# Rotary embedding of 16 x 512 x 1024 floats: the last tile stored in two pieces, and three small transfers in place of four

## The chip, the core and the metric

The kernel runs on one core of a Trainium2 chip. The time is device microseconds of one execution. Times inside a run ("at 147.6 us") count from the start of the profiled span, which is some 1.8 us shorter than the time of the run.

A transfer is cut into packets, which 16 DMA engines carry side by side; the last store of the kernel before is 128 packets of 32 KB, eight for each engine. A transfer has landed when each engine, after its packets, has counted up the semaphore of the transfer, a counter that other instructions wait for. A store is issued when SyncE hands it to its queue; its packets move when the engines come to them.

## The reference

```python
def reference(x, cos, sin, num_heads):          # shortened; x: 16 x 512 x 1024 float32, 16 heads of 64
    x = x.reshape(batch, seq, num_heads, head_dim)
    x1, x2 = x[..., :half_dim], x[..., half_dim:]
    # cos, sin: 512 x 32, broadcast over batch and heads
    return np.concatenate([x1 * cos - x2 * sin, x1 * sin + x2 * cos], axis=-1)
```

The input is 33.6 MB and so is the output. Each byte has to be moved once in each direction, 67.1 MB in all.

## The kernel before

The work is cut into eight tiles of 128 partitions. A partition holds eight rows of 1024 floats, so a tile is 4.19 MB. Five tile buffers are loaded at once; the last three loads wait until a buffer has been stored. All loads and stores are issued by SyncE and share one queue. Rows 0 and 3 are added on TensorE and copied by ScalarE; rows (1, 2), (4, 5) and (6, 7) are summed on VectorE in pairs; GpSimd makes the sine products.

```python
FIRST = (2, 3, 8)      # first tile: pieces of 2, 1 and 5 rows
LAST_OUT = (8,)        # last tile: stored whole
EXTRA = 4              # small transfers
...
    load(0, 0, FIRST[0])
    ...                                        # cos and sin tables, on ScalarE's queue
    for lo, hi in zip(FIRST, FIRST[1:]):
        load(0, lo, hi)
    for t in range(1, BUFS):
        load(t)
    spare = fixed.tile([1, EXTRA, 16], FP32)
    for i in range(EXTRA):                     # 64 bytes each, read by nobody
        nc.sync.dma_start(out=spare[:1, i], in_=sin_v[:1, :16])
...
    def stores(t):
        lo = 0
        for hi in LAST_OUT if t == NT - 1 else (KK,):
            store(t, lo, hi)
            lo = hi
        if t + 1 == NT - BUFS:
            for n in range(BUFS, NT):
                load(n)
...
        pair_sum(*p2, b2)                      # rows 4, 5
        pe_half(ROW_PE, *h1)                   # second half of row 3
        p1 = pair_product(t, third[0])         # rows 6, 7
        ...
        pair_sum(*p1, b1)
        stores(t)
```

The small transfers carry nothing that is used. They turn the sequence of semaphores: the transfers use eight semaphores in turn, and a transfer is not issued before the one eight places earlier has landed (in the trace of before the first landed at 5.91 us and the ninth was issued at 5.92).

Of the kernel before, what the change touches and what calls it, by code (L numbers as in the profile page):

```python
# [19 lines left out]
PAIRS = ((1, 2), (4, 5), (6, 7))  # L20

FIRST = (2, 3, 8)
LAST_OUT = (8,)

EXTRA = 4


@with_exitstack
def kernel(
# [40 lines left out]
    def load(t, lo=0, hi=KK):  # L70
        if tiles[t] is None:
            tiles[t] = xp.tile([P, F], FP32, name="xt")
        s = slice(lo * dim, hi * dim)
        nc.sync.dma_start(out=tiles[t][:, s], in_=x_v[t][:, s])

    def store(t, lo=0, hi=KK):
        s = slice(lo * dim, hi * dim)
        nc.sync.dma_start(out=out_v[t][:, s], in_=tiles[t][:, s])
# [9 lines left out]
# [3 lines that stand above are left out]
    for i in range(EXTRA):  # L91
        nc.sync.dma_start(out=spare[:1, i], in_=sin_v[:1, :16])
# [98 lines left out]
# [4 lines that stand above are left out]
# [64 lines left out]
```

## Time and profile before

| | |
|---|---|
| time, median of 3 runs | 162.48 us (162.30 to 162.54) |
| profiled span | 160.4 us |
| last sum on VectorE ends | 147.52 us |
| last store issued, landed | 147.59, 159.57 us |
| the store before it, landed | 149.92 us |
| moved over the span | 67.25 MB, mean 419 GB/s |
| busy share VectorE, GpSimd | 85%, 79% |

On the DMA row a packet's whole duration is booked in the slice in which the packet starts.

### The profile page before, as it was taken

To read this page: it belongs to the slowest core of one execution; us is meant where nothing else is said; L and a number is where in the kernel's file an instruction comes from. 1 tells how busy PE (TensorE), PEld (TensorE's weight loads), DVE (VectorE), ACT (ScalarE), POOL (GpSimd) and SP (SyncE) were. 2 spreads that over 40 slices of the span, in tenths; PEclk is the share of its full clock that TensorE was granted. 3 is DMA by queue.
4 is the path that set the end of the run, shared out by engine and by line. 5 is a ranking of instruction groups with operands and counts; after the bars stand their busy time and mean duration, and the time that the engine had idled before them with its cause. 6 is when DMAs were issued, how large, how long until landed. Compare 5 with 4: busy or idle time off the path is not lost.

```text
span 160.4 us, 444 instructions
## 1 busy us (share of the span) xinstructions
PE 57.0 (36%) x71; PEld 18.1 (11%) x71; DVE 136.3 (85%) x85; ACT 18.7 (12%) x25; POOL 127.1 (79%) x38
## 2 busy tenths in 40 slices
PE   3323705076305830293009320852057203930000
PEld 0102201031002200130004000300021002200000
DVE  1079879999999999999999999999999999997000
ACT  0003301003100310021100310031003100220000
POOL 1059999999999999988998799989989899830000
PEclk9999965556755585559555865567555855595555
DMA  5999999999999999999999999999999999999993
GB/s 176 413 414 469 400 515 392 392 474 441 392 441 449 417 392 458 458 392 433 476 400 425 482 400 400 490 409 400 466 433 409 441 458 409 433 466 409 409 474 163
DMA packets 2761, 67.25 MB, mean 419 GB/s; under 512 B 328, under 2 KB 456, under 8 KB 584
## 3 DMA queue, kind: packets, MB, share of 16 engines
q1 hardware_dynamic: 2600, 67.11, 97.8%
q10 hardware_dynamic: 160, 0.13, 0.3%
q14 instruction: 1, 0.01, 0.0%
HBM read 33.69 MB, written 33.55 MB: 419 GB/s over the span
## 4 chain that ended last, share of the span: by engine, by line
DVE 68%; issue 11%; POOL 7%; DMA 4%; PE 1%; ACTq 0%; DVEq 0%
DVE xt L189 33%; DVE pd L141 31%; POOL b L165 7%; DMA b<-in_cos_dram 4%; DVE pe_ps L141 4%; PE tab L114 1%; ACTq L84 0%; DVE sns L116 0%; DVE xt L150 0%; DVE own_ps L141 0%; DVE sns L117 0%; DVEq L189 0%
## 5 line engine op out<-in xcount | busy, mean ns | idle before, releaser
L165 POOL TENSOR_TENSOR b<-xt,sns 128x2048 f32<-128x2048 f32 (+1 forms) x32 | 126.4, 3978 | 14.0 <-DVE sns L117 8.6
L189 DVE TENSOR_TENSOR xt<-pd,b 128x2048 f32<-128x2048 f32 x24 | 54.9, 2287 | 2.4 <-POOL b L165 1.6
L141 DVE TENSOR_TENSOR pd<-xt,tab 128x2048 f32<-128x2048 f32 x24 | 55.0, 2292 | 0.2
L176 PE MATMUL own_ps<-xt,ident 128*128 128x512 f32 x32 | 30.1, 1095 | 59.4 <-DVE xt L150 53.7
L176 PE MATMUL pe_ps<-b,ident 128*128 128x512 f32 x32 | 24.7, 864 | 22.6 <-DVE pe_ps L141 22.6
L176 PEld LDWEIGHTS own_ps<-xt,ident 128*128 128x128 f32 x32 | 9.4, 324 | 75.2 <-DVE xt L150 60.5
L209 ACT COPY xt<-own_ps 128x1024 f32<-128x1024 f32 x8 | 8.1, 1012 | 78.6 <-PE own_ps L176 78.6
L181 ACT COPY xt<-pe_ps 128x512 f32<-128x512 f32 x16 | 9.4, 586 | 32.8 <-PE pe_ps L176 32.8
L176 PEld LDWEIGHTS pe_ps<-b,ident 128*128 128x128 f32 x32 | 7.4, 253 | 42.9 <-DVE pe_ps L141 34.4
L141 DVE TENSOR_TENSOR pe_ps<-xt,tab 128x512 f32<-128x512 f32 x16 | 11.0, 685 | 0.0
L141 DVE TENSOR_TENSOR own_ps<-xt,tab 128x1024 f32<-128x1024 f32 x8 | 9.8, 1223 | 0.0
L150 DVE TENSOR_TENSOR xt<-xt,tab 128x1024 f32<-128x1024 f32 x8 | 9.7, 1214 | 0.0
L116 DVE TENSOR_SCALAR sns<-tab 128x256 f32<-128x256 f32 x1 | 0.4, 425 | 7.5 <-PE tab L114 7.5
L209 ACT ACT_TABLE_LOAD x1 | 1.3, 1283 | 14.7 <-DVE xt L150 14.7
L113 PE MATMUL tab<-b,spread 64*128 64x256 f32 x2 | 1.2, 697 | 3.4 <-DMA b<-in_sin_dram 3.4
L101 PE MATMUL own_ps<-zero 128*128 128x512 bf16 x2 | 1.0, 622 | 1.2 <-DVE zero L97 1.2
L114 PE MATMUL tab<-b,spread 64*128 64x256 f32 x2 | 1.2, 710 | 0.5 <-DMA b<-in_cos_dram 0.5
L97 DVE MEMSET zero<- 128x256 uint32 x1 | 0.3, 272 | 0.9 <-PEq L240 0.9
L113 PEld LDWEIGHTS tab<-b,spread 64*128 64x128 f32 x2 | 0.5, 310 | 4.3 <-issue 4.3
L114 PEld LDWEIGHTS tab<-b,spread 64*128 64x128 f32 x2 | 0.5, 306 | 1.3 <-DMA b<-in_cos_dram 1.3
L101 PE MATMUL pe_ps<-zero 128*128 128x512 bf16 x1 | 0.6, 634 | 0.0
L101 PEld LDWEIGHTS <-zero 128*128 128x128 bf16 x3 | 0.3, 125 | 1.5 <-DVE zero L97 1.2
(9 smaller groups left out, 1.8 us busy)
## 6 DMA issues: line engine op xcount, KB each, us to landing
out_dram<-xt SPq DMA_DIRECT2D x8, 4096.0 KB, 21.9
xt<-in_x_dram SPq DMA_DIRECT2D x7, 4096.0 KB, 30.0
xt<-in_x_dram SPq DMA_DIRECT2D x1, 2560.0 KB
xt<-in_x_dram SPq DMA_DIRECT2D x1, 1024.0 KB
xt<-in_x_dram SPq DMA_DIRECT2D x1, 512.0 KB
b<-in_sin_dram ACTq DMA_DIRECT2D x1, 64.0 KB, 5.2
b<-in_cos_dram ACTq DMA_DIRECT2D x1, 64.0 KB
spare<-in_sin_dram SPq DMA_DIRECT2D x4, 0.1 KB
```

The source lines that it names most:

```text
L97: nc.vector.memset(zero, 0.0)
L101: nc.tensor.matmul(out=ps, lhsT=zero[:, :P], rhs=zero, start=True, stop=True)
L113: nc.tensor.matmul(out=sin_t, lhsT=spread, rhs=sin_sb, start=True, stop=True)
L114: nc.tensor.matmul(out=cos_t, lhsT=spread, rhs=cos_sb, start=True, stop=True)
L116: nc.vector.tensor_scalar_mul(out=sns[:, :, 0, :], in0=sin_k, scalar1=-1.0)
L141: nc.vector.tensor_tensor(out=o, in0=i, in1=cb, op=ALU.mult)
L150: nc.vector.tensor_tensor(out=heads(r), in0=heads(r), in1=s, op=ALU.mult)
L165: nc.gpsimd.tensor_tensor(out=o, in0=i, in1=sb, op=ALU.mult)
L176: nc.tensor.matmul(out=ps, lhsT=ident, rhs=other, start=False, stop=True, skip_group_check=True)
L181: nc.scalar.copy(out=r, in_=pe_ps)
L189: nc.vector.tensor_tensor(out=r, in0=ps, in1=b, op=ALU.add)
L209: nc.scalar.copy(out=r0, in_=own_ps)
```

## The change

The intent of the split is to let half of the last tile leave when rows 0 to 3 are ready, while the last pair of rows is still being computed. One small transfer is dropped, so that there are again 24 transfers and the last one is again on the last of the eight semaphores.

```diff
 FIRST = (2, 3, 8)
-LAST_OUT = (8,)
-
-EXTRA = 4
+LAST_OUT = (4, 8)
+
+EXTRA = 3
```

## The prediction

> **What bounds the kernel now.** I read the page's span and DMA lines first, because the change only touches transfers.
>
> ```profile
> span 160.4 us, 444 instructions
> ...
> DMA  5999999999999999999999999999999999999993
> ...
> q1 hardware_dynamic: 2600, 67.11, 97.8%
> ...
> DVE 68%; issue 11%; POOL 7%; DMA 4%; PE 1%; ACTq 0%; DVEq 0%
> ```
>
> The DMA row is at 9 in every slice but the first and the last, and the queue that SyncE feeds takes 97.8% of what 16 engines have in the span. The chain that ended last tells another story, 68% VectorE and 4% DMA. These are different questions: the chain follows releases back from the last work on an engine, and no engine's work has to wait for the end of the last store. So I asked when the queue could have run dry. Stretches first (columns: the stretch, its length, busy us of PE, PEld, DVE, ACT and POOL with their counts, PE clock, DMA share, GB/s):
>
> ```profile
> 2.00:147.50 145.50, 56.20 (x70) 17.84 (x68) 135.75 (x83) 18.66 (x25) 126.40 (x32) 0.65 1.00 429
> 147.50:149.90 2.40, 0.00 (x0) 0.00 (x0) 0.03 (x1) 0.00 (x0) 0.00 (x0) 0.50 0.98 423
> ```
>
> From 2 us until the arithmetic ends at 147.5 us the DMA engines are busy all the time, at 429 GB/s, and they still are for the 2.4 us after it. The end of the timeline, then SyncE's line with the store before it (issue at 131.54; two stores merged in one line), then the time from issue to landing of the one and the other, from the list of DMA issues in a window around 131.5 and around 147.6 us:
>
> ```profile
> 140.04 2.29 DVE L189 TENSOR_TENSOR xt<-pd,b 128x2048 f32<-128x2048 f32 x1
> ...
> 144.15 0.59 ACT L181 COPY xt<-pe_ps 128x512 f32<-128x512 f32 x1 [3.05 <-PE pe_ps L176]
> 145.23 2.29 DVE L189 TENSOR_TENSOR xt<-pd,b 128x2048 f32<-128x2048 f32 x1
> 147.59 0.33 SPq L78 DMA_DIRECT2D out_dram<-xt  x1
> ```
> ```profile
> 131.54 16.38 SPq L78 DMA_DIRECT2D out_dram<-xt  x2
> ```
> ```profile
> out_dram<-xt SPq DMA_DIRECT2D x1, 4096.0 KB, 18.4
> ```
> ```profile
> out_dram<-xt SPq DMA_DIRECT2D x1, 4096.0 KB, 12.0
> ```
>
> The store before the last is issued at 131.54 and lands 18.4 us later, at 149.9. The last is issued at 147.59 and lands 12.0 us later, at 159.6. The two landings are 9.7 us apart, and 4.19 MB in 9.7 us is 432 GB/s: the full rate of this queue. So of the 12.0 us, about 2.3 us are queueing behind the store before it, and the rest is movement at full speed. The semaphore records of the trace say the same of every 4 MB transfer: landings at 23.3, 33.0, 42.7, 52.6, 62.4, 72.0, 82.2, 91.9, 101.1, 110.8, 120.5, 130.2, 140.3, 149.9 and 159.6 us, in the order of issue, 9.2 to 10.2 us apart. The packet records of the last two stores have each engine going from one 32 KB packet (1.213 us) to the next with no gap, across the border between the stores, which the engines cross between 148.7 and 149.5 us. The kernel is a **full DMA queue from 1.8 us to 159.6 us**; bytes decide the end.
>
> Last, SyncE's own waits over the whole run:
>
> ```profile
> SPq L78 <- DVE xt L189: 112.2, 7, 16.6
> SPq L74 <- DMA out_dram<-xt: 16.7, 2, 9.7
> SPq L254 <- DMA out_dram<-xt: 11.4, 2, 9.6
> SPq L92 <- DMA xt<-in_x_dram: 5.3, 1, 5.3
> ```
>
> L92 is the small transfers, one of which holds SyncE 5.3 us; L254 is the end of the program, which waits 9.6 us for the last store.
>
> **What the Trainium skill says.** The Trainium skill, "DMA: Bandwidth & Descriptors", section "Queues, rings and completion order": on each engine descriptors are taken in ring order, and all that SyncE issues shares one row of rings. The landings above, all in issue order, agree; so a store issued earlier behind a full queue doesn't start moving earlier than its predecessors leave. Same page, section "Bandwidth": 16 ports at 32 B and 850 MHz give 435 GB/s; the 429 GB/s above is 99% of it, so no reordering can make the middle faster. Same page, "Why small descriptors are slow": a fixed cost for each packet. The packet records agree: 4096 B take 159 ns and 32,768 B take 1213 ns, so 1054 ns for 28,672 B, 0.0368 ns a byte, and 159 - 151 = 8 ns fixed. "Perfetto Trace Analysis", section "DMA Optimizations", says that splitting may let some transfers start sooner "if DMA engines are generally idle". Here they are not, at the one place where the split is made.
>
> **The change part by part.** The description also names the tables on ScalarE's queue and the first tile in pieces of two, one and five rows; both are in the kernel before, and the diff leaves them. Only two constants change.
>
> Last store in two. Rows 0 to 3 of the last tile are ready when the second half of row 3 has been copied: 144.15 + 0.59 = 144.74 us (rows 1 and 2 were summed by 137.1, row 0 copied by 139.9). Rows 6 and 7 are ready at 145.23 + 2.29 = 147.52. So the first piece is issued at about 144.8, 2.8 us earlier than now, and the second at 147.6 as now. But the store before occupies the engines until 148.7 to 149.5 (landing 149.9). The first piece, 2.1 MB, lands at about 149.9 + 4.85 = 154.8, the second at about 159.6. Removed from the end: 0. Added: on each engine 16 packets of 16 KB in place of 8 of 32 KB, so 8 x 8 ns = 0.065 us, and one more 4-byte semaphore packet, which with the step to it costs some 15 ns in the packet records. Together +0.08 us.
>
> One small transfer fewer. The fourth small one waits for the last piece of the first tile, which lands at 13.6 us; that is the 5.3 us wait above. Without it SyncE is free at about 8.3 rather than 13.8 us, and its next order is the first store at 29.7 us, which waits for VectorE. Worth 0. Its own 64 bytes (11 ns on one engine) and semaphore packet go: -0.02 us at most.
>
> Which semaphore each transfer uses moves. The trace shows eight semaphores in turn over all 24 transfers; a transfer waits until the one eight before it has landed. There are again 24 (3 small, 9 stores), so the last transfer again has the last of the eight. Stores 1 to 3 now follow the last piece of tile 0 (13.6), load 1 (23.3) and load 2 (33.0), and are issued at 29.7, 46.7 and 63.6; the loads at 64.1, 72.1 and 82.2 follow load 3 (42.7), load 4 (52.6) and a small one; the later stores follow small ones and stores that landed over 30 us before. The two pieces follow the third store (82.2) and the load that landed at 91.9. Nothing binds: 0.
>
> Sum: 0 + 0.08 - 0.02 + 0 = +0.06 us. On the median of before, 162.48, I take **162.5 us**.
>
> **The rivals.** *The exposed tail.* If one reads the last 12.0 us as a store with nothing beside it, half of it can go 2.8 us earlier and only 2.1 MB remain after 147.6: 4.85 us of movement plus about 2 us of latency, so an end 5 us earlier and some 157.5 us. For it: the digit rows of the engines are empty at the end, and the chain stops at VectorE. Against it: the DMA share of 0.98 from 147.5 to 149.9, the 9.7 us between landings, and above all the bytes: 67.1 MB at 432 GB/s need 155.4 us after a start at 1.8, so 157.2 at the earliest, and the kernel ends 2.4 us over that. Even with everything moved ideally it can't win 2%. I give it 1%.
>
> *A new wait by the moved semaphores.* If I have the turn wrong by one and a load is held until a transfer that is still queued, the queue could run dry: one such hole can cost up to a transfer's 9.7 us, 172 us at worst. Against it: every predecessor named above landed at least 13 us before the issue that would wait for it, with 20 us or more in the loads. 1%.
>
> *Smaller packets lose rate.* If 16 KB packets on the HBM side ran 2% slower, the last store would take 0.2 us more: 162.7. The 20 KB packets of the first tile are at 762 to 766 ns, 26.8 GB/s an engine against 27.0, so a per-cent effect on 4 MB, 0.1 us. Inside my range.
>
> *The queue was only just full.* The fastest engine left the earlier store at 148.7, 1.1 us after the last issue. If unprofiled runs are nearer to running dry, an earlier first piece helps a few tenths: 162.2. Also in the range.
>
> **Range and chances.** The three runs of before lie within 0.24 us, and my terms are under 0.1 us, so what is left is a different chip or hour: 162.1 to 163.0. Two per cent is 3.25 us, more than all of the kernel's DMA idle time together; hence 0.01 faster, 0.98 within 2%, 0.01 slower.
>
> **What would show it.** Right: DMA row all 9 as now; first piece issued near 144.8 and landing about 10 us later, second issued near 147.6 and again landing about 12.0 us later; three waits of the last line on the stores (about 2, 5 and 5 us) in place of two, with much the same sum; the 5.3 us wait of L92 gone and nothing moved by it. Wrong: a landing of the second piece under 10 us after its issue (the tail was exposed), a new wait of L74 or L78 on a DMA, or a DMA slice below 9 in the middle.

## The result

The changed kernel took 162.69 us (median of 6 runs, 162.26 to 162.79). The kernel before took 162.51 us beside it (6 runs, 162.30 to 162.82). The ratio is 1.0003, with a 95% interval of 0.9986 to 1.002: the same. Ratios here are the mean time of one kernel's fast runs over that of the other's of the same rounds, so they are not quite the ratio of the medians quoted.

The page of the changed kernel (span, DMA row, SyncE's queue with packets, MB and share, and the chain):

```profile
span 161.0 us, 444 instructions
...
DMA  5999999999999999999899999999999999999993
...
q1 hardware_dynamic: 2742, 67.11, 97.5%
...
DVE 68%; issue 11%; POOL 6%; DMA 4%; PE 1%; ACTq 0%; DVEq 0%
```

The queue is as full as before: 97.5% against 97.8%, with the same bytes. It has 142 packets more, which come from the 16 KB pieces: 128 data packets and 16 for the semaphore of the added store, less two of the dropped small transfer. The chain still reads 68% VectorE.

The stretches of the changed kernel up to the end of the arithmetic and just after it (the last two columns are DMA share and GB/s):

```profile
2.00:147.50 145.50, 55.74 (x70) 17.79 (x68) 135.55 (x83) 18.56 (x25) 126.43 (x32) 0.65 1.00 430
147.50:149.90 2.40, 0.00 (x0) 0.00 (x0) 0.21 (x1) 0.00 (x0) 0.00 (x0) 0.50 0.94 403
```

The end of the timeline, then SyncE's line of the last three stores:

```profile
145.28 0.59 ACT L181 COPY xt<-pe_ps 128x512 f32<-128x512 f32 x1 [5.14 <-PE pe_ps L176]
145.42 2.29 DVE L189 TENSOR_TENSOR xt<-pd,b 128x2048 f32<-128x2048 f32 x1
```
```profile
131.73 16.34 SPq L78 DMA_DIRECT2D out_dram<-xt  x3
```

The first piece was issued at 145.89 us, as soon as the second half of row 3 had been copied (145.28 + 0.59), and the second at 147.74. Their times from issue to landing, in the windows around 145.5 and around 148 us:

```profile
out_dram<-xt SPq DMA_DIRECT2D x1, 2048.0 KB, 9.4
```
```profile
out_dram<-xt SPq DMA_DIRECT2D x1, 2048.0 KB, 12.4
```

This is the whole result in two lines. The second piece is half the size of the old last store, was issued at the same place in the program, and took 12.4 us to land where the whole store took 12.0. A piece of 2.1 MB needs 4.85 us of movement at 432 GB/s; most of the rest is waiting. By the packet records the engines left the store before at 148.65 to 150.10 us and the first piece at 153.51 to 154.96, so the first piece began to move 2.8 to 4.2 us after its issue and the second 5.8 to 7.2 us after its own. The first piece was issued earlier and stood in the same queue.

SyncE's waits of the changed kernel:

```profile
SPq L78 <- DVE xt L189: 103.6, 7, 21.4
SPq L74 <- DMA out_dram<-xt: 16.6, 2, 9.9
SPq L78 <- ACT xt L181: 13.8, 1, 13.8
SPq L254 <- DMA out_dram<-xt: 11.9, 3, 4.8
```

The wait of 5.3 us for the first tile's last piece (L92) has gone from the list and no load or store has a new wait for a transfer. The end of the program (L254) now waits three times, 11.9 us in all, in place of twice, 11.4 us.

The prediction named a DMA slice below 9 in the middle as a sign against it, and the row above has an 8 in the twentieth slice. I checked it against the packet records. With each packet spread over its own time, every slice but the first and the last is at 1.00 to 1.02, in both kernels, and 16 packets or one more are under way at any moment around that slice. The 8 is the booking by start described above, not idle time.

The profiled run of the changed kernel ends 0.6 us later than that of before (landing at 160.17 against 159.57). The traces give another reason than the change. In both the packets of one of the 16 engines can be followed back from the last landing, and it is the engine that carried the one 8 KB packet of the instruction queue ("q14 instruction: 1" on the page of the kernel before) near 78.6 us: 0.309 us for it, and the data packet after it took 1.571 in place of 1.213 us. In the changed kernel's run this engine lost another 0.43 us in one packet near 109.7 us. Its last packet ended at 159.84, the next engine's at 159.05. In the run of before the two were at 159.21 and 159.04. The lengthened packet near 109.7 is no mark of the change either: the run of before has six packets of 1.29 to 1.47 us near 108.7 to 109.2. Other runs of the changed kernel had the shorter span: 160.5 us in two of six.

The other traces bear this out. In all eight in which the queue stayed full to the end (but for a few ns), the engine that ended last is the one with the instruction packet, 0.2 to 0.8 us after the next. In the three in which the queue ran dry before the last store or its first piece, the last two engines ended within 0.03 us of each other. No run removed that packet, so the link is read from traces and not tested.

### The profile page after: what moved, and what is told of

Its sections match the earlier page's. It is cut to its first block, busy times and chain, and to the rows that moved or that the text cites. A ratio compares the mean times of both kernels' runs of the same rounds, so it can differ in the third digit from the quotient of the medians.

```text
span 161.0 us, 444 instructions
## 1 busy us (share of the span) xinstructions
PE 56.6 (35%) x71; PEld 18.1 (11%) x71; DVE 136.3 (85%) x85; ACT 18.6 (12%) x25; POOL 127.1 (79%) x38
## 3 DMA queue, kind: packets, MB, share of 16 engines
q1 hardware_dynamic: 2742, 67.11, 97.5%
## 4 chain that ended last, share of the span: by engine, by line
DVE 68%; issue 11%; POOL 6%; DMA 4%; PE 1%; ACTq 0%; DVEq 0%
DVE xt L189 33%; DVE pd L141 31%; POOL b L165 6%; DMA b<-in_cos_dram 4%; DVE pe_ps L141 4%; PE tab L114 1%; ACTq L84 0%; DVE sns L116 0%; DVE xt L150 0%; DVE own_ps L141 0%; DVE sns L117 0%; DVEq L189 0%
## 5 line engine op out<-in xcount | busy, mean ns | idle before, releaser
L209 ACT COPY xt<-own_ps 128x1024 f32<-128x1024 f32 x8 | 8.1, 1012 | 78.6 <-PE own_ps L176 78.6
## 6 DMA issues: line engine op xcount, KB each, us to landing
xt<-in_x_dram SPq DMA_DIRECT2D x1, 2560.0 KB, 11.9
```

Of the source, the lines that this page charges most:

```text
L209: nc.scalar.copy(out=r0, in_=own_ps)
```

## Experiments

My theory: the queue is full until after the last store is ready, so only bytes (and the slowest engine) set the end, and moving an issue earlier within a full queue moves nothing. The main rival: the last store is exposed, and the split should win several microseconds, which something in the change then takes back (smaller packets, one more completion, a semaphore wait from the new turn). Nine experiments were run, one of them the changed kernel once more. Eight were made on one chip in two jobs of four; the 12 runs of before beside the second four include the 11 beside the first. The last of the table was made on another chip with runs of before of its own.

| run | median us (runs) | ratio to before | 95% interval |
|---|---|---|---|
| changed kernel again | 162.45 (6) | 1.0007 | 0.9988 to 1.0027 |
| split only | 162.28 (6) | 0.9995 | 0.9978 to 1.0013 |
| three small ones only | 162.32 (6) | 0.9997 | 0.9978 to 1.0015 |
| no small ones | 162.42 (6) | 1.0012 | 0.9988 to 1.0035 |
| late, stored whole | 166.30 (6) | 1.0245 | 1.0204 to 1.0286 |
| late, split | 162.38 (6) | 0.9995 | 0.9978 to 1.0012 |
| half loads, stored whole | 161.25 (6) | 0.9931 | 0.9909 to 0.9953 |
| half loads, split | 159.66 (6) | 0.9813 | 0.9782 to 0.9845 |
| 1 MB more | 164.86 (4) | 1.0154 | 1.0121 to 1.0186 |

### The parts, one at a time

The changed kernel once more:

> The changed kernel once more, beside the others on one chip, as the measure of what a tenth of a per cent means here. Full-queue theory: within 0.2% of the kernel before (0.998 to 1.002), single runs between 162.2 and 162.8 us, the difference between runs going with how late the slowest of the 16 DMA engines ends. Exposed-tail theory: 0.97, about 157.5 us.

It took 162.45 us against 162.28 for before (11 runs). In its profiled run (162.99 us) the tables came late, TensorE started on the cosine table at 9.58 in place of 7.97 us, and everything after it ran 1.6 us later, to a last sum ending at 149.32. The first piece was then issued at 147.50. Its slowest engine ended at 160.04, 0.7 us after the next.

The split alone:

```diff
-LAST_OUT = (8,)
+LAST_OUT = (4, 8)
 EXTRA = 4
```

> The last store in two pieces, but four small transfers as before. Full-queue theory: 162.5 us, ratio 1.000 to 1.001: 16 packets of 611 ns in place of 8 of 1213 ns on each engine are +0.07 us, and the second piece, now on the first of the eight semaphores, should cost at most 0.2 us at the end of the program. Exposed-tail theory: the gain of the split would show here at full size, 157.5 us, ratio 0.97. If the third small transfer had to go for the split to work, this run would be slower than the changed kernel by over 0.3%.

It took 162.28 us, ratio 0.9995. So the change does not consist of a gain by the split and a loss by the rest: the split alone is worth nothing here. Its last landing is on the first of the eight semaphores, and SyncE's wait at the end of the program is a single one:

```profile
SPq L254 <- DMA out_dram<-xt: 11.3, 1, 11.3
```

The span ended 0.86 us after the last landing, against 0.83 in the changed kernel: the order of the semaphores at the end costs nothing that one look can show.

Three small transfers alone:

```diff
 LAST_OUT = (8,)
-EXTRA = 4
+EXTRA = 3
```

> Three small transfers, the last store whole. Full-queue theory: 162.5 us, ratio 0.999 to 1.001: the wait of 5.3 us of SyncE for the last piece of the first tile is gone and SyncE issues nothing earlier for it. Theory that SyncE's wait costs something: up to 5.3 us less, 157.2 us. Theory that the moved semaphores make a load wait for a transfer still in the queue: a new wait of several us in SyncE's waits, and 2% or more added.

It took 162.32 us, ratio 0.9997. The 5.3 us that SyncE no longer waits were spent at a time when it had nothing to issue.

No small transfer, with the split:

```diff
-EXTRA = 3
+EXTRA = 0
-    spare = fixed.tile([1, EXTRA, 16], FP32)
-        nc.sync.dma_start(out=spare[:1, i], in_=sin_v[:1, :16])
+        pass
```

> The changed kernel without any small transfer. Full-queue theory: 162.5 us, ratio 0.999 to 1.001; SyncE's waits for the small transfers (6.6 us in all in the changed kernel and before) go and nothing follows. Theory of the semaphores' turn (that the count of small transfers keeps the last store on the last semaphore, or keeps a load from waiting): this run slower than the changed kernel, by 0.2 us or more at the end of the program, or by several us in a new wait of a load.

It took 162.42 us, ratio 1.0012, with one run at 163.41; the same within the interval. SyncE's list of waits has a new line, which I had not expected:

```profile
SPq L78 <- DMA xt<-in_x_dram: 1.2, 1, 1.2
```

It lies before the first store, which SyncE then issued at 29.94 us as in the other kernels (29.90 in the changed one), so it costs nothing. Here the span ended 1.02 us after the last landing, 0.19 us more than in the changed kernel. This fits a small price for a last transfer in the middle of the turn, but it is one look, and the times do not resolve it.

### Is the queue the limit? One megabyte more in the middle

```diff
-    spare = fixed.tile([1, EXTRA, 16], FP32)
+    spare = fixed.tile([P, EXTRA, 512], FP32)
-        nc.sync.dma_start(out=spare[:1, i], in_=sin_v[:1, :16])
+        nc.sync.dma_start(out=spare[:, i], in_=x_v[0][:, i * 512 : (i + 1) * 512])
```

> The kernel before, with the four small transfers of 64 bytes made 262 KB each, 1.05 MB in all, placed where they are now. Full-queue theory: 1.05 MB at 432 GB/s is 2.4 us, in the middle of the kernel, and the end moves by as much: 164.9 us, ratio 1.015. Theory of the chain of waits (68% VectorE, 4% DMA): the arithmetic still ends near 147.5, and a transfer in the middle is hidden: 162.5 us, ratio 1.000.

It took 164.86 us against 162.34, and the ratio is 1.0154. In its trace the arithmetic ends at 147.97 us, 0.45 us later than in the profiled run of before (147.52), and the last store is issued at 148.03:

```profile
145.68 2.29 DVE L189 TENSOR_TENSOR xt<-pd,b 128x2048 f32<-128x2048 f32 x1
148.03 0.33 SPq L78 DMA_DIRECT2D out_dram<-xt  x1
```

The chain of VectorE came 0.45 us later, yet the kernel is 2.5 us longer, which is what 1.05 MB take at 432 GB/s (2.4 us). Bytes set the end.

### What the split does when the arithmetic is late

In both kernels the product of the last tile's last pair was done three times. That is idempotent, so the results are correct, and the last sum comes about 4.6 us later (it began at 150.14 us in both traces, against 145.42 in the changed kernel).

```diff
-        p1 = pair_product(t, third[0])
+        for _ in range(3 if t == NT - 1 else 1):
+            p1 = pair_product(t, third[0])
```

Stored whole:

> The kernel before, with the product of rows 6 and 7 of the last tile done three times in place of once, so that its last sum ends 2 x 2.29 = 4.6 us later, near 152.1 us. Full-queue theory: the last store is issued at 152.2, the engines have run dry at about 149, its first packet starts 1.0 us after the issue, 9.7 us of movement and 0.4 to the landing follow: landing near 163.3 in place of 159.6, so +3.7 us, about 166.2 us, ratio 1.023. Theory that VectorE's chain sets the end one for one: +4.6 us, 167.1, ratio 1.028.

Stored in two pieces:

> The changed kernel with the same 4.6 us put before its last sum. Full-queue theory: the first piece (issued near 145) keeps the engines busy until about 153.9 (the fastest), the second is issued at 152.2 and its packets can start at 153.2, so nothing is lost: 162.5 to 162.8 us, ratio 1.000 to 1.003, and 2.2% under the whole store with the same delay. Theory that VectorE's chain sets the end, with or without a split: 167 us.

The times were 166.30 and 162.38 us. The stretches of the whole store, then of the split one (DMA share and GB/s at the end of each line):

```profile
147.50:149.90 2.40, 0.00 (x0) 0.00 (x0) 2.37 (x2) 0.00 (x0) 0.00 (x0) 0.50 0.48 205
149.90:153.50 3.60, 0.00 (x0) 0.00 (x0) 2.43 (x2) 0.00 (x0) 0.00 (x0) 0.50 0.34 146
```
```profile
147.50:149.90 2.40, 0.00 (x0) 0.00 (x0) 2.37 (x2) 0.00 (x0) 0.00 (x0) 0.50 0.97 416
149.90:153.50 3.60, 0.00 (x0) 0.00 (x0) 2.43 (x2) 0.00 (x0) 0.00 (x0) 0.50 1.01 432
```

Stored whole, the store was issued at 152.50; by the packet records the engines had run out of packets between 148.7 and 149.7 and started again at 153.3, and the last landing came at 163.59, 4.0 us after that of before. Stored in two, the first piece (issued at 145.01) bridged the gap: the queue stayed full although VectorE was 4.6 us late, and the time is that of the undelayed kernel. So the split does work as a mechanism. What it gives is slack, 4.6 us of it at least, for which the kernel before had no use.

How near to running dry the kernel before was can be worked out. Its last store was issued at 147.59 us. Into an idle queue the first packet moves 0.83 us after the issue, and the last of the 16 engines starts at 0.98 (last section). So the store could have moved from 148.42 on, and the first engine left the earlier store at 148.71: a margin of at most 0.3 us. The slowest engine left it at 149.52. The run with three small transfers and a whole store shows the edge itself: issued at 147.91, the store moved at 148.74, and a few engines then stood idle for a few ns each, 0.09 us in all. In the changed kernel the same working gives 153.51 - (147.74 + 0.83) = 4.9 us. The slack gained is thus about the movement of the first piece, 4.85 us.

The spread fits this: the runs of the whole store went from 165.58 to 167.81, those of the split one from 162.13 to 162.40.

### What the split does when the queue is not full

In both kernels only rows 0 to 3 of the last three tiles were loaded, into the buffer of the tile five places earlier, whose old contents stand in for the other rows. The results of those tiles are wrong. This takes 6.3 MB off the queue and leaves the arithmetic as it was.

```diff
-            tiles[t] = xp.tile([P, F], FP32, name="xt")
+            tiles[t] = tiles[t - BUFS] if t >= BUFS else xp.tile([P, F], FP32, name="xt")
...
-                load(n)
+                load(n, 0, 4)
```

Stored whole:

> The kernel before, with only half of each of the last three tiles loaded (into the buffer of the tile five before; the results of those tiles are wrong on purpose): 6.3 MB less, 14.6 us of the queue at 432 GB/s. Full-queue theory: the queue runs dry before the last store, which then starts 1.0 us after its issue at 147.6 and lands near 158.7: 161.4 us, ratio 0.993 to 0.996; DMA slices below 9 in the second half. Nothing like the 14.6 us is won, because the arithmetic ends at 147.5 and 4.2 MB remain. A theory in which bytes alone set the end: 148 us.

Stored in two pieces:

> The changed kernel with the same halved loads (wrong on purpose). Full-queue theory: with an idle queue the first piece starts moving when it is ready, 144.8 to 145.9, so the end comes 1.7 to 2.8 us before that of the whole store with the same loads: 158.6 to 159.7 us, ratio to the kernel before 0.976 to 0.983. Theory that the split is worth nothing in itself (two pieces cost what they win): the same time as the whole store with halved loads, 0.993 to 0.996.

The times were 161.25 and 159.66 us, a difference of 1.6 us. The stretches before and after the last issue, for the whole store and then for the split one:

```profile
144.00:147.50 3.50, 0.78 (x1) 0.00 (x0) 3.14 (x2) 0.59 (x1) 0.00 (x0) 0.50 0.00 0
147.50:158.00 10.50, 0.00 (x0) 0.00 (x0) 0.00 (x0) 0.00 (x0) 0.00 (x0) 0.50 0.93 399
```
```profile
144.00:147.50 3.50, 0.00 (x0) 0.00 (x0) 3.04 (x2) 0.35 (x1) 0.00 (x0) 0.51 0.71 300
147.50:158.00 10.50, 0.00 (x0) 0.00 (x0) 0.00 (x0) 0.00 (x0) 0.00 (x0) 0.50 0.71 300
```

With an idle queue before the last store (share 0.00), the first piece moves at once (share 0.71 in the same stretch), and the split wins what the exposed-tail theory promised in kind, though 1.6 us and not five: the gain is limited by how long rows 0 to 3 are ready before the rest. In the profiled runs the first piece was issued at 144.38 and the whole store at 147.31, 2.9 us apart, and the landings at 155.57 and 158.39 are 2.8 us apart. That run of the split (158.19 us) was the fastest of its six; over all of them the gain is 1.6 us. The issue of the first piece lay between 144.4 and 145.9 us in five of the traces here and at 147.5 in the one with late tables, so a first piece that is ready later in the slower runs would explain the smaller mean; those runs have no trace, and it stays argued. Part of the cause is in the traces: the two matmuls of the second half of row 3 took 1.12 us in the profiled split run, at a granted TensorE clock of 1.00, and 2.07 us in the run of the whole store, at 0.50. That moves the first piece by 0.95 us. Taking 14.6 us of bytes away from the whole store won only 1.0 us (161.25 against 162.24): the arithmetic takes over as the limit almost at once. The two limits lie that close together. (The ratios are 0.9931 and 0.9813, and the intervals do not touch.)

## Why the prediction was right

Predicted were 162.5 us and 162.1 to 163.0, with 0.98 for within 2%; measured were 162.69 us and a ratio of 1.0003. By its steps:

- **Full queue until after the last store is ready.** Right, and shown: one megabyte in the middle moved the end by its own duration, and with 6.3 MB less the queue ran dry and the split began to pay.
- **Removed from the end: 0.** Right, and shown by the split alone (0.9995) and by the 12.4 us landing of the second piece.
- **First piece issued at about 144.8.** It was issued at 145.89 in the changed kernel's trace. The two matmuls of row 3's second half took 2.07 us together in that run, where the run of before had 1.13, so the copy came later. The granted clock is the reason: in the run of before it was 1.00 from 140.9 to 144.3 us, over the whole of these matmuls (142.98 to 144.11), while in the changed kernel's run the stretch at 1.00 had ended at 141.5 and they ran at 0.50. Over the traces it is the same: 1.12 to 1.13 us in the four in which the clock was 1.00 throughout, 2.07 to 2.08 in the four in which it was 0.50, and between these where it changed on the way. The prediction took their time from one trace as fixed. In the split-only run it was 145.51, in the half-load run 144.38. The term was mis-sized and, in a full queue, worth nothing.
- **Smaller packets, +0.065 us.** The size was right: the 16 KB packets took 611 ns, so 8 x (2 x 611 - 1213) = 72 ns more on each engine. The 159 ns that the prediction took for 4 KB is the shortest of those packets; their median in that trace is 189 ns. The times cannot show 0.07 us, the intervals are some 0.3 us to either side.
- **One small transfer fewer, 0.** Right: three small ones alone gave 0.9997.
- **Semaphores' turn, 0.** Right: no load or store was held in the changed kernel (the prediction's "20 us or more in the loads" is 19.5 us for one of them, 72.1 less 52.6), and with no small transfers at all the time is the same within 0.35%.
- **The rivals.** The exposed tail falls for this kernel; the half-load pair shows the condition under which it would hold. Nothing of a new wait was seen. Its "about 2 us of latency" is also high: 0.83 us from issue to first packet, and 0.37 us from the last packet to the landing in the run of before, make 1.2 us. That the queue was only just full is right, and more so than the prediction said: its 1.1 us left out the 0.83 us before a packet moves, which leaves at most 0.3 us on the first engine. Whether the split saves a few tenths in the runs in which the tables come late stays open, since the runs of the changed kernel scatter as much (162.26 to 162.99; before 162.13 to 163.10). An estimate from the profiled run with late tables speaks against it. Stored whole at 149.35, the tile would have moved on every engine by 150.33 and needed 9.7 us, to 160.0; the slowest engine there left the store before at 150.30 and ended at 160.0 anyway.

No version with correct results was clearly faster than both kernels. After a start at 1.8 us the bytes alone need until 157.2 us at 432 GB/s; the landing is at 159.6 to 160.2. Between the two lie small packets at the start, packets that took longer than 1213 ns (13 near 50.4 us in the run of before, by 0.3 us on average), the lag of the slowest engine, and the 0.37 us to the landing; how the rest divides among them was not worked out.

## What to carry to other kernels

Before you split a last store, look whether the queue is empty when the first piece is ready: compare the landing of the store before it with the issue of the last one, and allow for the time from an issue to its first packet (0.83 us here). If that landing comes later, the split buys slack against a late last sum, about as much as the first piece takes to move, and no time; if it comes earlier, the split wins at most the time by which the first piece is ready before the second. And read the chain of waits together with the DMA row: a chain that is two thirds VectorE said nothing about the end of this kernel, while adding a known number of bytes settled it in one run.

## What the Trainium skill lacked or had wrong

- "DMA: Bandwidth & Descriptors", section "Bandwidth": its note that the HBM side (about 358 GB/s) binds transfers between HBM and on-chip memory is too general. It leaves out the condition that stands further up in the same section, that both cores of a pair are streaming. This one core moved loads and stores together at 429 to 430 GB/s for 145 us, near the page's fabric figure of 435.
- The same page, "Why small descriptors are slow", gives the fixed cost of a packet as about 3 cycles, besides 32 bytes of descriptor data, with 256 bytes as its only worked case and no time in ns. For large packets the records of these runs show 309, 611 and 1213 ns for 8, 16 and 32 KB (medians) and 159 ns for the shortest of 4 KB: 8 to 9 ns fixed each, so halving 32 KB packets costs 0.7%.
- "Perfetto Trace Analysis", section "DMA Optimizations", offers splitting as a way to an earlier end when DMA engines are generally idle, which they were not where this split was made. It lacks the other use: under a full queue the split bought slack, 166.30 against 162.38 us with the last sum 4.6 us late.
- "Runtime: NRT & Kernel Launch", section "Instruction fetch mechanics", tells that instructions are fetched by DMA during a run and calls the cost mostly hidden. What a fetch costs a full data queue is not in any page that I found. One 8 KB instruction packet near 80 us took 0.309 us of one engine, and that engine's next packet took 0.36 to 0.61 us longer than 1.213; in all eight traces with a full queue that engine ended last, by 0.2 to 0.8 us.
- "DMA: Bandwidth & Descriptors", section "Latency and other measured facts", gives about 0.6 us to the first byte for transfers issued by SyncE and does not say from where it counts. Into an idle queue the first packet began 0.83 us after the start of the issue in three runs here (152.50 to 153.33, 147.31 to 148.14, 144.38 to 145.21 us), of which the issue itself is 0.33; the last of the 16 engines began at 0.98.
